# Indexer heads summed pair by pair as they are projected, and a query block's mask moved from a matrix product to GpSimd

## The chip, the cores and the metric

The kernel runs on one core of one Trainium2 chip. The metric is the device time of one execution in microseconds (us). Shorter is better. Engines are named as the profile names them: PE (matrix products), PEld (its weight loads), DVE (vector engine), ACT (scalar engine), POOL (GpSimd), SP (sync engine, which issues loads).

## What is computed

A trunk of two layers over 512 positions of width 1024: a gated linear recurrence, a feed-forward with a short convolution, a sparse attention, a second feed-forward, a final norm. The change lies in the sparse attention alone. Its reference, cut to what matters:

```
dots = jnp.einsum('bthd,bsd->bths', qib, k_idx)                       # 8 index heads of 64
scores = jnp.einsum('bths,bth->bts', jax.nn.relu(dots), wb)           # weighted sum over the heads
scores = jnp.where(admissible[None], scores, NEG_BIG)                 # causal
_, sel = lax.top_k(scores, top_k)                                     # top_k = 128 of up to 512 keys
logits = jnp.einsum('btkgd,btskd->btkgs', qb, k_sel) * (ATT_HEAD_DIM ** -0.5)
probs = softmax(where(valid, logits + bias, NEG_BIG))                 # 16 heads, relative-position bias
out = einsum('btkgs,btskd->btkgd', probs, v_sel)
```

The kernel gathers nothing. It computes all logits of a query block and adds a large number to the keys that were not selected.

## The kernel before

All work is in blocks of 128 queries (t = 0 to 3); block t sees (t + 1) * 128 keys. Every float32 product is made of three products of parts, so a projection of 128 columns (`proj_T`) is 8 steps of three matrix products, 24 in all. Weights pass through `wunit`: SP loads them, ACT writes the high part `whi` (L143 or L159) and ACT, DVE or POOL the low part `wlo`; in one form (L158 to L160) ACT writes a negated copy and POOL issues a load that adds to it. The buffers of `whi` and `wlo` are three deep.

The attention stage begins with the index key (KI, 72 columns: 64 of the key, 8 head weights), then four projections of the index queries (QI0 to QI3 here, two heads each; `head_in`), then K, V and eight pairs of query heads (q0 to q7; `rest_in`). `kw_evac` (L704 to L706) makes the two parts of the index key, and `kw_weights` transposes the head weights on PE (`pw`) and has DVE write `wN` (L715). After each QI projection `stack` splits its result into the two parts of both heads: ACT writes halves of `qh` and `ql` (L675, L676), DVE the other halves (L677, L678).

`dots` then runs for t = 1, 2, 3 and, inside that, for the four pairs of index heads: four matrix products into two banks `pi` (L749), a ReLU on ACT (L759) and a multiply-add on DVE into the score tile `sc[t]`, a part of `scs` (L755 and L760). POOL masks the diagonal block (L762). `top` finds the 128 largest by 16 rounds of MAX8 and MATCH_REPLACE8 on DVE (L774, L776), first for t = 1, then for t = 2 and 3, and writes the mask `sel[t]` (L779).

The attention itself goes in units (hf, b): head pair b and query blocks 0, 1 (hf = 0) or 2, 3 (hf = 1); six hf = 0 units come first, then both kinds mixed. `products` multiplies queries by keys into banks `pl` (L863). For t = 1 and t = 2 PE first adds the mask by a product of `sel[t]` with the identity (L860). For t = 3 POOL has added mask and bias beforehand (`mask3`, L833) into `scs`, which is free by then. `biased` (L870) is one DVE pass that adds the bias, or bias and mask, and takes the row minimum. ACT exponentiates (L889); `mixv` transposes the probabilities on PE (L912, L915), ACT copies them out (L916), and PE multiplies them by the values (L923, L926).

What sets the order: on PE the program's own order is kept. Pieces of work that run beside a projection are generators given to `add_side`; `weave` advances them by the PE time each step is reckoned at. The order on the other engines is made by the scheduler from when it reckons each operation ready, and each engine then works strictly through its own list.

Of the kernel before, what the change touches and what calls it, by code (L numbers as in the profile page):

```python
# [8 lines left out]
F32 = mybir.dt.float32  # L9
# [3 lines left out]
AF = mybir.ActivationFunctionType  # L13
ALU = mybir.AluOpType
# [3 lines left out]
P = 128  # L18
D = 1024
T = 512  # L20
# [3 lines left out]
NEG = -1e30  # L24
# [24 lines left out]
def trunk(ctx: ExitStack, tc: tile.TileContext, xT, vecs, convs, hgrn_w_in, hgrn_w_out, dsa_w_in, dsa_w_out,  # L49
# [11 lines left out]
    def bank(name):  # L61
        return ps.tile([P, 512], F32, name=name, tag="bank")
# [124 lines left out]
    def add_side(gen, rate=1.0):  # L187
        side.append([gen, rate, 0.0])
# [472 lines left out]
    with ExitStack() as sx:  # L661
# [9 lines left out]
        def stack(b, src, lo):  # L671

            a, c = qh[:, b, :], ql[:, b, :]
            top_, bot = rows2
            nc.scalar.activation(a[top_], src[top_], AF.Copy)  # L675
            nc.scalar.activation(c[bot], src[bot], AF.Copy)  # L676
            lo.tensor_tensor(a[bot], src[top_], a[top_].bitcast(F32), op=ALU.subtract)  # L677
            lo.tensor_tensor(c[top_], src[bot], c[bot].bitcast(F32), op=ALU.subtract)  # L678
# [9 lines left out]
        with ExitStack() as sy:  # L688
# [20 lines left out]
            def kw_weights():  # L709
                tmp = kw.pop()  # L710
                pw = bank("pw")
                for t in range(TT):
                    nc.tensor.transpose(pw[:, t * 72:(t + 1) * 72], tmp[:72, t * P:(t + 1) * P], ident[:72, :72])
                for t in range(TT):
                    nc.vector.tensor_scalar(wN[:, t, :], pw[:, t * 72 + 64:(t + 1) * 72], 8 ** -0.5 * 64 ** -0.5,  # L715
                                            rstd_c[:, t:t + 1], op0=ALU.mult, op1=ALU.mult)

            def setup():

# [13 lines left out]
            def head_in():  # L733
                pk = yield from proj_T(w_in, O_KI, 72)
                for b in range(4):
                    o = yield from proj_T(w_in, O_QI + b * P,
                                          hook=({7: lambda: kw_evac(pk)}, {2: kw_weights}, None, None)[b])
                    lo_engine[0] = nc.gpsimd
                    stack(4 + b, o, nc.vector)

            def dots():
                for t in range(1, TT):
                    w = (t + 1) * P
                    ts_ = slice(t * P, (t + 1) * P)
                    for b in range(4):
                        o = [bank("pi") for _ in range(2)]
                        for k_ in (ki_h, ki_l):
                            for e in range(2):
                                nc.tensor.matmul(o[e][:, :w], (qh, ql)[e][:, 4 + b, ts_], k_[:, :w],  # L749
                                                 start=k_ is ki_h, stop=k_ is ki_l)  # L750
                        yield 0.22 * (t + 1)
                        for e in range(2):
                            i = 2 * b + e
                            if i == 0:
                                nc.vector.tensor_scalar(sc[t], o[e][:, :w], 0.0, wN[:, t, 0:1],  # L755
                                                        op0=ALU.max, op1=ALU.mult)
                            else:
                                r_ = ix.tile([P, T], F32, name="relu", bufs=2)
                                nc.scalar.activation(r_[:, :w], o[e][:, :w], AF.Relu)  # L759
                                nc.vector.scalar_tensor_tensor(sc[t], r_[:, :w], wN[:, t, i:i + 1], sc[t],  # L760
                                                               op0=ALU.mult, op1=ALU.add)
                    nc.gpsimd.affine_select(sc[t][:, w - P:], sc[t][:, w - P:], pattern=[[-1, P]], base=0,  # L762
                                            channel_multiplier=1, compare_op=ALU.is_ge, fill=NEG)
                    done.add(f"sc{t}")
                    if t == 1:
                        add_side(top((1,)), 0.4)

            def top(ts):

                while any(f"sc{t}" not in done for t in ts):  # L770
                    yield 0.5
                for r in range(16):
                    for t in ts:
                        nc.vector.max(m8[:, t, :], sc[t])  # L774
                    for t in ts:
                        nc.vector.match_replace(sc[t], m8[:, t, :], sc[t], -3e38)  # L776
                    yield sum(2 * (0.065 + (t + 1) * P / 960) for t in ts)
                for t in ts:
                    nc.vector.tensor_scalar(sel[t], sc[t], -2e38, -NEG, op0=ALU.is_gt, op1=ALU.mult)  # L779
                    done.add(f"sel{t}")  # L780
                if 3 not in ts:
                    add_side(top((2, 3)), 0.55)
# [29 lines left out]
            add_side(norm_chain())  # L812
            add_side(setup())
            weave(head_in())
            add_side(dots(), 1.0)
            rest = rest_in()
            for c in rest:
                weave([c])
# [3 lines left out]
        at = sx.enter_context(tc.tile_pool(name="at", bufs=2))  # L822
        probs = {}

        def masked(b, e):
            return scs[:, e * T:e * T + T]

        def mask3(b):

            if b < KB and f"m{b}" not in done:  # L830
                done.add(f"m{b}")
                for e in range(2):
                    nc.gpsimd.tensor_tensor(masked(b, e), bias[:, 2 * b + e, :], sel[3], op=ALU.add)  # L833

        def scores(u):


            hf, b = u
            g = b // 4
            tiles = (2 * hf, 2 * hf + 1)  # L840
            if hf == 0:
                pb = [bank("pl") for _ in range(2)]
                ps_ = {(t, e): pb[e][:, t * 256:t * 256 + 256] for t in tiles for e in range(2)}
            else:
                ps_ = {}
            mn = [at.tile([P, 2], F32, name="mn", bufs=6) for e in range(2)]
            L = [[None, None], [None, None]]

            def products(t):
                w = (t + 1) * P  # L850
                wp = max(w, 256)
                ts_ = slice(t * P, t * P + P)
                if hf:
                    for e in range(2):
                        ps_[t, e] = bank("pl")
                if t == 3:
                    mask3(b)
                elif t:
                    for e in range(2):
                        nc.tensor.matmul(ps_[t, e][:, :w], identb, sel[t], start=True, stop=False)  # L860
                for k_ in (kh, kl):
                    for e in range(2):
                        nc.tensor.matmul(ps_[t, e][:, :wp], (qh, ql)[e][:, b, ts_], k_[g][:, :wp],  # L863
                                         start=t in (0, 3) and k_ is kh, stop=k_ is kl)

            def biased(j, t):
                w = (t + 1) * P
                for e in range(2):
                    L[e][j] = at.tile([P, 384 + j * P], F32, name=f"L{j}", bufs=4)
                    nc.vector.tensor_tensor_reduce(L[e][j][:, :w], ps_[t, e][:, :w],  # L870
                                                   masked(b, e) if t == 3 else bias[:, 2 * b + e, (3 - t) * P:],
                                                   scale=1.0,
                                                   scalar=3e38, op0=ALU.add, op1=ALU.min,
                                                   accum_out=mn[e][:, j:j + 1])

            for j, t in enumerate(tiles):
                products(t)
                if hf:
                    biased(j, t)
                yield (0.47, 0.66, 0.87, 0.92)[t]  # L880
            if hf == 0:
                for j, t in enumerate(tiles):
                    biased(j, t)
            sm = at.tile([P, 2, 2], F32, name="sm", bufs=4)
            rs = at.tile([P, 2, 2, 64], F32, name="rs", bufs=4)
            for e in range(2):
                for j, t in enumerate(tiles):
                    l = L[e][j][:, :(t + 1) * P]
                    nc.scalar.activation(l, l, AF.Exp, bias=mn[e][:, j:j + 1], scale=-1.0, accum_out=sm[:, j, e:e + 1])  # L889
            nc.vector.reciprocal(sm, sm)  # L890
            nc.vector.tensor_copy(rs, sm[:, :, :, None].to_broadcast([P, 2, 2, 64]))
            probs[u] = L, rs
            if {"sel3", "q8"} <= done:
                later = [c for f, c in units[units.index(u) + 1:] if f]
                mask3(later[0] if later else KB)
# [143 lines left out]
```

## Time and profile before

| | us |
|---|---|
| median of three runs | 1273.68 (1273.42 to 1275.24) |
| the profiled execution's own time | 1276.48 |
| its span, first to last instruction | 1274.7 |
| PE busy | 1251.4 (98%) |
| DVE busy | 803.0 (63%) |
| ACT busy | 599.6 (47%) |
| POOL busy | 138.8 (11%) |

The attention stage lies at 668 to 865 us of the span. Busy time is the union of an engine's instructions. A PE that is busy all the time in a stretch has no waits there; the time is then the sum of what it issues.

### The profile page before, as it was taken

Reading aid. Unit: us, or ns where it says so; the run is one execution under the profiler, and the core shown is the slowest. Engines: PE = TensorE matmul, PEld = TensorE weight load, DVE = VectorE, ACT = ScalarE, POOL = GpSimd, SP = SyncE. Lnnn points to the kernel's source line nnn. Section 1 sums busy time; section 2 is a strip of 40 time slices with the busy share of each in tenths; the row PEclk is TensorE's granted clock in tenths of the full one; section 3 lists DMA queues with packets and bytes.
Section 4 is the critical chain, followed back from the end, with each engine's and each line's share of the span. In section 5 each row is a group of like instructions: output and inputs, shape, how many; then the busy total and the mean of one; then the engine's idle time right before and its main releaser. Section 6 shows DMA issues by size and latency. Waiting matters only on the chain.

```text
span 1274.7 us, 15695 instructions
## 1 busy us (share of the span) xinstructions
PE 1251.4 (98%) x6054; PEld 1046.2 (82%) x6054; DVE 803.0 (63%) x1305; ACT 599.6 (47%) x989; POOL 138.8 (11%) x120
## 2 busy tenths in 40 slices
PE   8999999999999999999999998999999999999997
PEld 7788888887888888888887777988888888888887
DVE  7755777756777777742444999635677777762331
ACT  5546565444544444421337757853444444441430
POOL 3022223110000000000003453300000000000000
PEclk9999999999999999999999999999999999999999
DMA  6339777323333333322237850003233333333222
GB/s 199 117 73 158 133 129 126 76 66 99 91 93 98 99 99 99 98 91 93 87 103 173 134 109 25 27 1 99 83 100 99 99 99 94 92 95 99 91 75 66
DMA packets 199178, 124.05 MB, mean 97 GB/s; under 512 B 5264, under 2 KB 188480, under 8 KB 199104
## 3 DMA queue, kind: packets, MB, share of 16 engines
q1 hardware_dynamic: 170320, 108.31, 28.7%
q0 software_dynamic: 28080, 14.16, 9.3%
q8 instruction: 47, 0.77, 0.3%
q10 hardware_dynamic: 704, 0.58, 0.2%
q14 instruction: 27, 0.22, 0.1%
HBM read 120.92 MB, written 2.12 MB: 97 GB/s over the span
## 4 chain that ended last, share of the span: by engine, by line
PE 88%; DVE 7%; ACT 2%; issue 1%; DMA 0%; POOL 0%; DVEq 0%; SPq 0%; POOLq 0%; ACTq 0%
PE pj L169 17%; PE pj L171 17%; PE pj L170 17%; PE px L169 9%; PE px L171 9%; PE px L170 9%; PE pav L923 2%; DVE scs L776 2%; PE pl L556 1%; PE po L602 1%; DVE m L774 1%; DVE scs L760 1%; PE pl L863 1%; PE pt L912 1%; PE pn L170 1%
## 5 line engine op out<-in xcount | busy, mean ns | idle before, releaser
L169 PE MATMUL pj<-x,whi 128*128 128x512 f32 (+1 forms) x1016 | 403.0, 397 | 0.0
L171 PE MATMUL pj<-x,wlo 128*128 128x512 f32 (+1 forms) x1016 | 396.9, 391 | 1.1 <-DMA wlo<-in_dsa_w_in_dram 1.1
L170 PE MATMUL pj<-x,whi 128*128 128x512 f32 (+1 forms) x1016 | 396.3, 390 | 0.0
L144 DVE TENSOR_TENSOR wlo<-wr,whi 128x1024 fp32r<-128x1024 f32 (+2 forms) x165 | 202.0, 1224 | 155.1 <-ACT whi L143 153.1
L143 ACT ACTIVATE whi<-wr 128x1024 fp32r<-128x1024 f32 (+1 forms) x167 | 173.6, 1039 | 257.1 <-PE px L170 155.2
L171 PEld LDWEIGHTS pj<-x,wlo 128*128 128x128 f32 (+1 forms) x1016 | 190.6, 188 | 42.4 <-DMA wlo<-in_dsa_w_in_dram 1.5
L169 PEld LDWEIGHTS pj<-x,whi 128*128 128x128 f32 (+1 forms) x1016 | 191.0, 188 | 39.2 <-issue 1.6
L170 PEld LDWEIGHTS pj<-x,whi 128*128 128x128 f32 (+1 forms) x1016 | 191.1, 188 | 38.8 <-issue 1.0
L169 PE MATMUL px<-ah,whi 128*128 128x512 f32 (+1 forms) x332 | 128.5, 387 | 0.0
L171 PE MATMUL px<-ah,wlo 128*128 128x512 f32 (+1 forms) x332 | 127.5, 384 | 0.0
L170 PE MATMUL px<-al,whi 128*128 128x512 f32 (+1 forms) x332 | 126.2, 380 | 0.0
L348 DVE TENSOR_TENSOR ub<-pj,rstd_r 128x512 f32<-128x512 f32 x88 | 60.6, 688 | 82.3 <-PE pj L171 77.3
L143 ACT ACTIVATE ah<-c 128x512 fp32r<-128x512 f32 x44 | 27.8, 631 | 115.9 <-DVE c L360 115.9
L171 PEld LDWEIGHTS px<-ah,wlo 128*128 128x128 f32 x332 | 62.3, 188 | 13.5
L170 PEld LDWEIGHTS px<-al,whi 128*128 128x128 f32 x332 | 62.3, 188 | 12.8
L351 ACT ACTIVATE c<-ub,convc 128x512 f32<-128x512 f32 x88 | 71.2, 809 | 2.4 <-DVE ub L348 1.6
L169 PEld LDWEIGHTS px<-ah,whi 128*128 128x128 f32 x332 | 62.4, 188 | 11.4
L353 DVE SCALAR_TENSOR_TENSOR c<-ub,convc,c 128x512 f32<-128x512 f32 x88 | 66.2, 752 | 3.0
L358 ACT ACTIVATE c<-c 128x512 f32<-128x512 f32 x44 | 27.8, 632 | 80.8 <-DVE c L353 80.7
L352 DVE SCALAR_TENSOR_TENSOR c<-ub,convc,c 128x512 f32<-128x512 f32 x88 | 65.6, 746 | 0.0
L522 DVE TENSOR_TENSOR qk<-qk,ftree 128x512 f32<-128x512 f32 x56 | 39.6, 709 | 17.6 <-PE pl L560 7.1
L144 DVE TENSOR_TENSOR al<-c,ah 128x512 fp32r<-128x512 f32 x44 | 30.4, 692 | 29.3 <-ACT ah L143 29.3
(226 smaller groups left out, 1743.9 us busy)
## 6 DMA issues: line engine op xcount, KB each, us to landing
wr<-in_ffn_w_up_dram SPq DMA_DIRECT2D x88, 512.0 KB, 3.8
wr<-in_ffn_w_down_dram SPq DMA_DIRECT2D x41, 512.0 KB, 3.7
wr<-in_hgrn_w_in_dram SPq DMA_DIRECT2D x30, 512.0 KB, 4.1
wlo<-in_hgrn_w_in_dram POOLq DMA_DIRECT2D x19, 512.0 KB, 7.5
wr<-in_dsa_w_in_dram SPq DMA_DIRECT2D x14, 512.0 KB, 3.7
wr<-in_hgrn_w_out_dram SPq DMA_DIRECT2D x8, 512.0 KB, 3.6
wlo<-in_dsa_w_in_dram POOLq DMA_DIRECT2D x8, 512.0 KB, 7.8
wr<-in_dsa_w_out_dram SPq DMA_DIRECT2D x8, 512.0 KB, 3.8
```

Source lines behind the costliest of these rows:

```text
L143: nc.scalar.activation(dst_h, src, AF.Copy)
L144: lo.tensor_tensor(dst_l, src, dst_h.bitcast(F32), op=ALU.subtract)
L169: nc.tensor.matmul(o, ah, bh, start=start, stop=False)
L170: nc.tensor.matmul(o, ah, bl, start=False, stop=False)
L171: nc.tensor.matmul(o, al, bh, start=False, stop=stop)
L348: nc.vector.tensor_tensor(u[:, 2:], o, rows(), op=ALU.mult)
L351: nc.scalar.activation(c, u[:, 2:], AF.Identity, scale=cc[2], bias=cc[3])
L352: nc.vector.scalar_tensor_tensor(c, u[:, 1:T + 1], cc[1], c, op0=ALU.mult, op1=ALU.add)
L353: nc.vector.scalar_tensor_tensor(c, u[:, 0:T], cc[0], c, op0=ALU.mult, op1=ALU.add)
L358: nc.scalar.activation(g, g, AF.Silu)
L522: nc.vector.tensor_tensor(turned(m), turned(m), factors(ft, m), op=ALU.mult)
L776: nc.vector.match_replace(sc[t], m8[:, t, :], sc[t], -3e38)
```

## The change

Two edits. First, `dots` becomes `dots(b)`: one piece of side work for each pair of index heads, added as soon as the `stack` of that pair has been issued, with the loop over t inside. It starts once `wN` has been issued. The masking of the diagonal and `top((1,))` follow the last pair. Second, the mask of query block t = 2 is added to the bias by POOL, as that of t = 3 already was, into two new tiles `m20` and `m21`; the product with the identity stays for t = 1 alone.

```diff
+                done.add("wN")
...
                     stack(4 + b, o, nc.vector)
-
-            def dots():
+                    add_side(dots(b))
+
+            def dots(b):
+
+                while "wN" not in done:
+                    yield 0.3
                 for t in range(1, TT):
...
-                    for b in range(4):
...
+                    if b == 3:
+                        nc.gpsimd.affine_select(sc[t][:, w - P:], sc[t][:, w - P:], pattern=[[-1, P]], base=0,
...
-            add_side(dots(), 1.0)
...
-        def masked(b, e):
-            return scs[:, e * T:e * T + T]
+        masked2 = [at.tile([P, 3 * P], F32, name=f"m2{e}", bufs=1) for e in range(2)]
+
+        def masked(t, e):
+            return scs[:, e * T:e * T + T] if t == 3 else masked2[e]
...
-                for e in range(2):
-                    nc.gpsimd.tensor_tensor(masked(b, e), bias[:, 2 * b + e, :], sel[3], op=ALU.add)
+                for t in (2, 3):
+                    for e in range(2):
+                        nc.gpsimd.tensor_tensor(masked(t, e), bias[:, 2 * b + e, (3 - t) * P:], sel[t], op=ALU.add)
...
-                if t == 3:
+                if t >= 2:
                     mask3(b)
...
-                                                   masked(b, e) if t == 3 else bias[:, 2 * b + e, (3 - t) * P:],
+                                                   masked(t, e) if t >= 2 else bias[:, 2 * b + e, (3 - t) * P:],
```

Where the projections of the second and third pair of index queries meet, PE's list before is (`pj_5136` is QI1's result, `pj_5184` QI2's):

```order
L169 MATMUL pj_5136<-x_79,whi_5132 128x512
L170 MATMUL pj_5136<-x_81,whi_5132 128x512
L171 MATMUL pj_5136<-x_79,wlo_5133 128x512
L169 MATMUL pj_5184<-x_78,whi_5180 128x512
L170 MATMUL pj_5184<-x_80,whi_5180 128x512
L171 MATMUL pj_5184<-x_78,wlo_5181 128x512
L169 MATMUL pj_5184<-x_78,whi_5180 128x512
L170 MATMUL pj_5184<-x_80,whi_5180 128x512
```

In the changed kernel the same place on PE (`pj_5136` is again QI1, `pj_5214` is QI2; `qh` and `ql` are what `stack` writes) is:

```order
L169 MATMUL pj_5136<-x_79,whi_5132 128x512
L170 MATMUL pj_5136<-x_81,whi_5132 128x512
L171 MATMUL pj_5136<-x_79,wlo_5133 128x512
L169 MATMUL pj_5214<-x_78,whi_5210 128x512
L170 MATMUL pj_5214<-x_80,whi_5210 128x512
L171 MATMUL pj_5214<-x_78,wlo_5211 128x512
L753 MATMUL pi_5222<-ki_h_5032,qh_5012 128x256
L753 MATMUL pi_5223<-ki_h_5032,ql_5013 128x256
L753 MATMUL pi_5222<-ki_l_5033,qh_5012 128x256
L753 MATMUL pi_5223<-ki_l_5033,ql_5013 128x256
L753 MATMUL pi_5234<-ki_h_5032,qh_5012 128x384
L753 MATMUL pi_5235<-ki_h_5032,ql_5013 128x384
```

The first product of pair 1 has come to stand three matrix products behind the end of its own projection; it stands in the same place behind QI2 and QI3, and for pair 0 three products behind the transposes `pw`. Before, the products of all pairs stood behind QI3 and three products of K.

On ACT, around the splits of those projections, the list before reads (L159 and L158 are weight parts, L675 and L676 the halves of `stack`):

```order
L159 ACTIVATE whi<-wr 128x1024
L675 ACTIVATE qh<-pj 64x512
L676 ACTIVATE ql<-pj 64x512
L158 ACTIVATE wlo<-wr 128x1024
L159 ACTIVATE whi<-wr 128x1024
L675 ACTIVATE qh<-pj 64x512
L676 ACTIVATE ql<-pj 64x512
```

And in the changed kernel:

```order
L675 ACTIVATE qh<-pj 64x512
L676 ACTIVATE ql<-pj 64x512
L158 ACTIVATE wlo<-wr 128x1024
L763 ACTIVATE relu<-pi 128x256 x2
L763 ACTIVATE relu<-pi 128x384 x2
L763 ACTIVATE relu<-pi 128x512 x2
L159 ACTIVATE whi<-wr 128x1024
L675 ACTIVATE qh<-pj 64x512
L676 ACTIVATE ql<-pj 64x512
```

The six ReLUs of a pair now stand between two splits, and the weight part L159 still stands ahead of each split.

On POOL, in the hf = 1 units, the difference begins with these rows (`m_5598` and `m_5599` are the new tiles):

```order
-L833 TENSOR_TENSOR scs<-bias,sel_5021 128x512 x16
-L344 MEMSET ub_7187 128x2
-L344 MEMSET ub_7188 128x2
+L840 TENSOR_TENSOR m_5598<-bias,sel_5020 128x384
+L840 TENSOR_TENSOR m_5599<-bias,sel_5020 128x384
+L840 TENSOR_TENSOR scs<-bias,sel_5021 128x512 x2
+L840 TENSOR_TENSOR m_5598<-bias,sel_5020 128x384
+L840 TENSOR_TENSOR m_5599<-bias,sel_5020 128x384
+L840 TENSOR_TENSOR scs<-bias,sel_5021 128x512 x2
```

Two additions of 384 columns now stand ahead of the two of 512 columns, eight times over.

## Rows read from the trace of the kernel before

**Rows 1.** Stretches: length; busy of PE, PEld, DVE, ACT, POOL; clock; DMA.
```profile
684.00:699.00 15.00, 15.00 (x69) 12.42 (x68) 7.78 (x12) 8.78 (x12) 4.85 (x3) 1.00 0.65 127
716.00:740.00 24.00, 22.30 (x101) 17.89 (x100) 24.00 (x68) 15.58 (x21) 12.79 (x11) 1.00 0.96 153
785.00:790.00 5.00, 3.23 (x23) 2.81 (x23) 4.55 (x17) 3.09 (x11) 0.86 (x1) 1.00 0.00 0
800.00:840.00 40.00, 40.00 (x258) 36.67 (x257) 24.10 (x88) 34.51 (x94) 13.68 (x12) 1.00 0.04 13
```

**Rows 2.** PE's waits at 668 to 850: total us, times, longest.
```profile
PE pl L860 <- DVE sel L779: 3.9, 2, 2.1
...
PE pj L171 <- DMA wlo<-in_dsa_w_in_dram: 1.1, 1, 1.1
...
PE pt L796 <- DVE tmp L696: 0.6, 1, 0.6
```

**Rows 3.** Timeline of PE: start, us, engine, line, operation.
```profile
684.75 0.40 PE L169 MATMUL pj<-x,whi 128*128 128x512 f32 x1
...
699.06 0.28 PE L749 MATMUL pi<-ki_h,qh 128*128 128x256 f32 x1
...
701.89 0.28 PE L749 MATMUL pi<-ki_h,qh 128*128 128x256 f32 x1
702.26 0.36 PE L749 MATMUL pi<-ki_h,ql 128*128 128x256 f32 x1
```

**Rows 4.** Timeline of ACT behind the end of QI3, with idle time and releaser.
```profile
698.41 1.06 ACT L159 ACTIVATE whi<-wr 128x1024 fp32r<-128x1024 f32 x1 [2.08 <-issue]
699.48 0.59 ACT L675 ACTIVATE qh<-pj 64x512 fp32r<-64x512 f32 x1
700.08 0.59 ACT L676 ACTIVATE ql<-pj 64x512 fp32r<-64x512 f32 x1
```

**Rows 5.** Timeline of DVE: the index key's low part, then splits of the first and last pair.
```profile
683.77 2.47 DVE L705 TENSOR_TENSOR ki_l<-tmp,ki_h 64x512 fp32r<-64x512 f32 x1 [0.77 <-ACT ki_h L704]
...
687.34 0.68 DVE L677 TENSOR_TENSOR qh<-pj,qh 64x512 fp32r<-64x512 f32 x1
688.06 0.69 DVE L678 TENSOR_TENSOR ql<-pj,ql 64x512 fp32r<-64x512 f32 x1
...
700.71 0.69 DVE L677 TENSOR_TENSOR qh<-pj,qh 64x512 fp32r<-64x512 f32 x1 [0.60 <-ACT ql L676]
701.42 0.69 DVE L678 TENSOR_TENSOR ql<-pj,ql 64x512 fp32r<-64x512 f32 x1
```

**Rows 6.** The stretch behind PE's wait for the first mask; columns as in Rows 1.
```profile
743.60:747.20 3.60, 3.60 (x11) 2.82 (x10) 2.92 (x13) 1.97 (x8) 0.17 (x1) 0.53 0.91 113
```

**Rows 7.** Timeline of PE at the mask products of two hf = 1 units.
```profile
822.58 0.49 PE L860 MATMUL pl<-sel,identb 128*128 128x384 bf16 x2
...
829.31 0.49 PE L860 MATMUL pl<-sel,identb 128*128 128x384 bf16 x2
829.50 0.47 PE L863 MATMUL pl<-kh,qh 128*128 128x384 f32 x1
829.81 0.34 PE L863 MATMUL pl<-kh,ql 128*128 128x384 f32 x1
829.98 0.34 PE L863 MATMUL pl<-kl,qh 128*128 128x384 f32 x1
```

**Rows 8.** DVE's first MAX8 and the mask of block t = 1.
```profile
707.33 0.41 DVE L774 MAX8 m<-scs 128x8 f32<-128x256 f32 x1
...
741.83 0.73 DVE L779 TENSOR_SCALAR sel<-scs 128x256 bf16<-128x256 f32 x1
```

**Rows 9.** Timeline of POOL: a weight part, and additions of mask and bias.
```profile
683.29 2.39 POOL L144 TENSOR_TENSOR wlo<-wr,whi 128x1024 fp32r<-128x1024 f32 x1 [3.58 <-ACT whi L143]
...
793.35 2.14 POOL L833 TENSOR_TENSOR scs<-bias,sel 128x512 f32<-128x512 f32 x1
...
832.12 2.27 POOL L833 TENSOR_TENSOR scs<-bias,sel 128x512 f32<-128x512 f32 x2 [4.07 <-DVE mn L870]
```

More of the change, by code (lines that the diff above doesn't have):

```diff
@@ L744, in dots @@
                     ts_ = slice(t * P, (t + 1) * P)
-                    for b in range(4):
-                        o = [bank("pi") for _ in range(2)]
-                        for k_ in (ki_h, ki_l):
-                            for e in range(2):
-                                nc.tensor.matmul(o[e][:, :w], (qh, ql)[e][:, 4 + b, ts_], k_[:, :w],
-                                                 start=k_ is ki_h, stop=k_ is ki_l)
-                        yield 0.22 * (t + 1)
-                        for e in range(2):
[L753 to L766, printed above, removed]
+                    o = [bank("pi") for _ in range(2)]
+                    for k_ in (ki_h, ki_l):
+                        for e in range(2):
+                            nc.tensor.matmul(o[e][:, :w], (qh, ql)[e][:, 4 + b, ts_], k_[:, :w],
+                                             start=k_ is ki_h, stop=k_ is ki_l)
@@ new lines, in dots @@
+                    yield 0.22 * (t + 1)
+                    for e in range(2):
+                        i = 2 * b + e
+                        if i == 0:
+                            nc.vector.tensor_scalar(sc[t], o[e][:, :w], 0.0, wN[:, t, 0:1],
+                                                    op0=ALU.max, op1=ALU.mult)
+                        else:
+                            r_ = ix.tile([P, T], F32, name="relu", bufs=2)
+                            nc.scalar.activation(r_[:, :w], o[e][:, :w], AF.Relu)
+                            nc.vector.scalar_tensor_tensor(sc[t], r_[:, :w], wN[:, t, i:i + 1], sc[t],
+                                                           op0=ALU.mult, op1=ALU.add)
@@ L768, in top @@
+                    if b == 3:
+                        nc.gpsimd.affine_select(sc[t][:, w - P:], sc[t][:, w - P:], pattern=[[-1, P]], base=0,
+                                                channel_multiplier=1, compare_op=ALU.is_ge, fill=NEG)
+                        done.add(f"sc{t}")
+                        if t == 1:
+                            add_side(top((1,)), 0.4)
             def top(ts):
@@ L831, in mask3 @@
                 done.add(f"m{b}")
-                for e in range(2):
-                    nc.gpsimd.tensor_tensor(masked(b, e), bias[:, 2 * b + e, :], sel[3], op=ALU.add)
+                for t in (2, 3):
+                    for e in range(2):
+                        nc.gpsimd.tensor_tensor(masked(t, e), bias[:, 2 * b + e, (3 - t) * P:], sel[t], op=ALU.add)
         def scores(u):
@@ L863, in products @@
                         nc.tensor.matmul(ps_[t, e][:, :wp], (qh, ql)[e][:, b, ts_], k_[g][:, :wp],
-                                         start=t in (0, 3) and k_ is kh, stop=k_ is kl)
+                                         start=t != 1 and k_ is kh, stop=k_ is kl)
             def biased(j, t):
```

## Prediction

> **What bounds the kernel now.** I read the stretches first, then PE's waits, then the timelines of the engines around each wait. In the heart of the attention PE has no gap, 40.00 of 40 us, while DVE has 24.10 and POOL 13.68 [rows 1]: what PE no longer issues there is saved, and what PE waits anywhere is paid, unless a later wait shrinks by as much. Ahead of it the picture is another one. From 684 to 699, while the index queries are projected, DVE has 7.78 of 15 us; from 716 to 740 it is full, 24.00 of 24, and PE has gaps [rows 1]. PE's waits in the stage that this change can touch are two for masks, 3.9 us in all with 2.1 the longer and so 1.8 the other, 1.1 for a weight part that comes by a POOL load, and 0.6 for a scaled projection [rows 2]. Behind the 2.1 us wait the granted clock was 0.53 for 3.6 us, close to the lower level of 1.2 GHz [rows 6]: 3.6 x (1 - 0.53) = 1.7 us lost. Behind the 1.8 us wait the clock stayed at 1.00 in the stretch at 785 [rows 1].
>
> **The first edit, what it adds.** Nothing is removed: the same 48 index products, ReLUs and multiply-adds are issued. What moves is PE's place for them, and PE keeps its list. They need `qh` and `ql` of their pair, and those have a chain. Behind the end of QI3, ACT first runs the weight part L159 from 698.41, which takes 1.06, and only then the two halves of the split, from 699.48 and 700.08 [rows 4]; DVE adds the other halves at 700.71 and 701.42, and `ql` is complete at 701.42 + 0.69 = 702.11 [rows 5]. PE's product with it starts at 702.26 [rows 3], so the signal takes 0.15. L159 writes the weight buffer that the finished projection has just freed, so it cannot come sooner, and in the changed list it still stands ahead of the split.
>
> Before, this latency lay under the other pairs' products. In the changed list the first product of a pair stands three products behind its projection, the place that PE reached at 699.06 [rows 3] behind QI3. There it must wait for `qh`: 700.71 + 0.69 + 0.15 = 701.55, or 2.5 us [rows 5]. The second product waits for `ql` until 702.26, which is 3.2 behind 699.06; less the one product of 256 columns in between, 0.12 us (by columns from the 0.17 that separates two of 384 [rows 7]; 0.23 for 512), the pair waits 3.1 us. The same three ACT and two DVE operations follow QI1 and QI2, so pairs 1, 2 and 3 pay 3 x 3.1 = 9.3.
>
> Pair 0 has another chain. Its products stand three products behind the transposes `pw`, a place that PE reached at 684.75 [rows 3]. Its split waits on DVE behind the low part of the index key, which took 2.47 us at 683.77 where its like takes 0.7, in the same time as a weight part on POOL from 683.29 to 685.68 [rows 5, 9]. So `qh` is there at 687.34 + 0.68 + 0.15 = 688.17, a wait of 3.4, and `ql` at 688.06 + 0.69 + 0.15 = 688.90, 0.6 behind its product's turn at 688.29 [rows 5]. Pair 0 pays 4.0. The four come to 13.3; before, the last pair already lost 702.26 - 701.89 = 0.37 less 0.12, so 0.25, in this way [rows 3]. **Added: 13.0.** Nothing covers it: PE's next rows are products that stand behind the waiting one, and ACT, DVE and POOL have nothing that would need less time for it.
>
> The clock: four waits of 3.1 to 4.0 us are each longer than the one of 2.1 that cost 1.7. Two waits of about 2 us disagree [rows 1, 6], so the number of falls is open, from none to five (four pairs and the first mask) against one before. I take three: **2 x 1.7 = 3.4 more**, bounds -1.7 and +6.8. The Trainium skill, "TensorE: Matmul & The Clock Gate", section "HAM oscillation — how this bites in real kernels", says that a loop with repeated waits pays the return to half clock at each of them, not once. By that the sum would be higher by the two further falls, 3.4; the trace agrees for one wait of two.
>
> **The first edit, what it gives back.** DVE's sums begin some 15 us sooner, in time that it had free, so less stands between its first MAX8 and the mask, 707.33 to 742.56 before [rows 8]. But PE's list from the last pair to the mask product is full as well, 120 projection products of 0.23 us = 28 us, and the last pair's sums are themselves late by the waits above. In the changed list DVE has 6 multiply-adds there instead of 14, but three MAX8 and four MATCH_REPLACE8 of the later blocks more. So the 2.1 us wait may stay or go: I take **-1.0**, bounds 0 and -2.1. The wait of 1.8 for the masks of t = 2 and 3 goes: three hf = 0 units instead of six stand ahead of them on DVE, and PE no longer needs them for its products, only DVE does, later: **-1.8**. The weight part that came 1.1 late was queued on ACT behind ReLUs that are no longer there, and the 0.6 came from the full DVE: **-1.2** of 1.7, bounds 0 and -1.7.
>
> **The second edit.** Per hf = 1 unit it takes a pair of mask products off PE. They start at 829.31, the next product at 829.50, and that one is followed after 0.31 where the next spacing is 0.17 [rows 7]: 0.19 + 0.14 = 0.33 if the slower start goes too, 0.19 if it stays behind the transposes. Eight units: 1.5 to 2.6, **-2.2**. POOL gets two additions of 384 columns. Two of 512 take 2.27 [rows 9], so by columns 0.86 each, 1.7 a unit and 4.0 in all; a unit takes PE 829.31 - 822.58 = 6.7 us, now 0.3 less [rows 7], and the masks of the next unit are made while PE transposes. I cost it at nothing while that holds.
>
> **Sum.** 13.0 + 3.4 - 1.0 - 1.8 - 1.2 - 2.2 = +10.2. The profiled execution took 1276.48 us, so its like would take 1286.7; against the median of 1273.68 shown for before, which is 2.8 lower for the same work, the forecast is 1283.9.
>
> **Rivals.** *The earlier sums win.* If the splits came in time, all that is left of the sum is its gains: -2.2 for the mask products, -3.9 for both mask waits, -1.7 for the clock and -1.7 for the rest, -9.5, and the time is 1264.2. It decides at an average wait of 9.5 / 4 = 2.4 us per pair: below that the kernel is faster. For it speaks the half-empty DVE at 684 to 699; against it that the row at 702.26 shows PE waiting for just this split although two other pairs' products and six projection products had stood between. 0.08. *No measurable change:* the waits come to about 2.4 each, or no clock falls and all gains are full with a few waits shortened, 1271 to 1276.2. 0.06.
>
> *POOL's masks come too late.* `m20`, `m21` and `scs` exist once, so the masks of a unit start only when DVE has read those of the last, and where two hf = 1 units follow each other without an hf = 0 unit between, little time is left. One addition took 2.14 instead of 1.14 us [rows 9]. If all four did so, a unit's masks would take 4.0 x 2.14 / 1.14 = 7.5, 1.1 above PE's 6.4, and six units in a row would add 6: 1290. The Trainium skill, "SBUF — State Buffer", section "Who interferes with whom", gives the mechanism: POOL and a DVE operation with two SBUF inputs lock each other out for a whole instruction. The row at 793.35 bears that out, but DVE's pass over `pl` has one input in PSUM and is not of that kind. 0.08.
>
> **How the numbers follow.** The forecast, with waits of 3 to 4 us at each pair, has 0.78, and lies between 13.0 - 1.7 - 2.6 - 1.8 - 2.1 - 1.7 = +3.1 and 13.0 + 6.8 - 1.5 - 1.8 = +16.5: 1276.8 to 1290.2. With a little of the neighbouring cases the range is 1276.5 to 1291; it leaves out the faster case, the unchanged one and the ends. 0.2% is 2.5 us, about what a measurement of this kernel can tell from no change. Slower by more: the forecast and POOL's case, 0.86. Within it: 0.06. Faster: 0.08.
>
> **What would show it.** In the profile after, PE should wait in front of L753 four times, for DVE L678 or L677, about 13 us in all, with stretches of lower clock behind some; DVE should have its gaps there too. The wait for the masks of t = 2 and 3 should be gone, POOL should have 32 additions, and PE should stay without gaps in the hf = 1 units. The forecast is wrong if PE's waits at L753 come to under 9 us, or if PE waits for transposes' inputs behind late masks.

## The result: slower by 18.1 us, at the upper end of the range

| | before | after |
|---|---|---|
| median, us | 1273.68 (1273.42 to 1275.24) | 1291.82 (1287.59 to 1293.63, 4 runs) |
| the profiled execution's own time | 1276.48 | 1292.92 |
| its span | 1274.7 | 1291.1 |
| PE busy | 1251.4 | 1258.9 |
| DVE / ACT / POOL busy | 803.0 / 599.6 / 138.8 | 808.4 / 599.2 / 150.7 |

The ratio is 1.0135, with a 95% interval of 1.0108 to 1.0162. The forecast was 1283.9 with a range up to 1291.0. The median lies 0.8 us beyond that end; the ratio, which goes by the means, gives 1273.68 x 1.0135 = 1290.9, just inside. Four runs do not tell the two apart. The sign and the main mechanism were right; the size was 1.7 to 1.8 times the forecast. Between the two profiled executions the difference is 16.4 us, and that is what the terms below are added up against.

PE's waits in the attention stage, in the profile of after (engine, line, tile, what it waited for, us in total, times, longest), which answer [rows 2]:

```profile
PE pi L753 <- DVE qh L677: 9.1, 4, 2.8
PE pt L922 <- DVE rs L898: 2.4, 1, 2.4
PE pl L867 <- DVE sel L784: 2.1, 1, 2.1
PE pav L930 <- ACT px L923: 1.5, 3, 1.0
PE pi L753 <- DVE ql L678: 1.3, 4, 0.4
```

The four waits in front of the index products are there, as foreseen. They come to 9.1 + 1.3 = 10.4 us, above the 9 below which the prediction called itself wrong. The wait for the masks of t = 2 and 3 is gone, and so are the late weight part and the late `tmp`. The 2.1 us for the mask of t = 1 stayed. And there is a wait that the prediction did not have: 2.4 us for `rs`, the reciprocal rows that PE transposes.

PE's timeline at pairs 0 and 2 (start, duration, instruction, and in brackets the idle time before it), which answers [rows 3]:

```profile
684.37 0.40 PE L171 MATMUL pj<-x,wlo 128*128 128x512 f32 x1
687.54 0.58 PE L753 MATMUL pi<-ki_h,qh 128*128 128x256 f32 x1 [2.77 <-DVE qh L677]
688.36 0.55 PE L753 MATMUL pi<-ki_h,ql 128*128 128x256 f32 x1 [0.23 <-DVE ql L678]
...
692.13 0.63 PE L753 MATMUL pi<-ki_h,ql 128*128 128x512 f32 x1
692.55 0.63 PE L753 MATMUL pi<-ki_l,qh 128*128 128x512 f32 x1
...
708.12 0.39 PE L171 MATMUL pj<-x,wlo 128*128 128x512 f32 x1
710.60 0.58 PE L753 MATMUL pi<-ki_h,qh 128*128 128x256 f32 x1 [2.10 <-DVE qh L677]
711.42 0.55 PE L753 MATMUL pi<-ki_h,ql 128*128 128x256 f32 x1 [0.23 <-DVE ql L678]
```

The bracket counts from the modelled end of the product ahead. What PE really loses is counted by starts: the product ahead starts at 708.12 and takes 0.23 of PE's time, so the place is reached at 708.35 and left at 710.60, 2.25 us; the next product stands 0.82 behind where it should stand 0.12 behind, 0.70 more. That makes 2.95 us for pair 2, and pairs 1 and 3 have the same two waits. Pair 0 loses 687.54 - 684.60 = 2.94 and 0.70, together 3.64. The four come to 3.64 + 3 x 2.95 = 12.5. The two rows at 692 show the other part of the loss: these products start 0.42 apart where 0.23 is usual.

The chain behind a wait is the one that the prediction had read from [rows 4, 5]. ACT at pair 2, in after:

```profile
707.69 1.06 ACT L159 ACTIVATE whi<-wr 128x1024 fp32r<-128x1024 f32 x1 [3.36 <-issue]
708.65 0.57 ACT L675 ACTIVATE qh<-pj 64x512 fp32r<-64x512 f32 x1
709.24 0.59 ACT L676 ACTIVATE ql<-pj 64x512 fp32r<-64x512 f32 x1
```

and DVE behind it, idle for 4.38 us until ACT's second half was done:

```profile
709.86 0.68 DVE L677 TENSOR_TENSOR qh<-pj,qh 64x512 fp32r<-64x512 f32 x1 [4.38 <-ACT ql L676]
```

The granted clock in the stretches behind the waits (window, length, busy time and instructions of PE, PEld, DVE, ACT and POOL, granted clock, DMA share, GB/s), which answer [rows 6]: behind pairs 0, 1, 2 and 3, behind the mask of t = 1, behind the wait for `rs`.

```profile
688.00:693.00 5.00, 4.76 (x15) 4.09 (x15) 2.78 (x7) 0.88 (x2) 0.00 (x0) 0.50 0.03 10
699.00:703.50 4.50, 4.28 (x15) 3.66 (x16) 2.28 (x5) 1.90 (x5) 1.61 (x1) 0.64 0.81 150
711.00:716.00 5.00, 4.76 (x14) 4.07 (x14) 2.47 (x5) 1.56 (x4) 1.55 (x1) 0.50 0.87 157
724.00:727.00 3.00, 2.60 (x9) 2.40 (x10) 1.53 (x3) 1.18 (x4) 1.55 (x1) 0.52 0.55 153
759.00:763.00 4.00, 3.77 (x20) 3.21 (x20) 4.00 (x17) 3.94 (x10) 2.65 (x3) 1.00 1.09 201
799.00:802.00 3.00, 2.68 (x12) 2.13 (x11) 3.00 (x14) 2.90 (x12) 0.00 (x0) 0.54 0.03 4
```

0.50 is the lower level, 1.2 GHz. It fell behind all four pairs and behind `rs`, five times, but not behind the 2.13 us for the mask, where the profile of before shows its one fall behind a wait of 2.14. The five did not cost the same. Counted by starts (each distance between products less what the same product takes at clock 1.00) the four pairs lost 2.4, 1.6, 2.8 and 1.4 us, 8.1 together, and the fall behind `rs` 1.3: behind pairs 0 and 2 the clock stayed low about twice as long as behind 1 and 3.

Where `rs` was late, DVE and POOL were at work at the same time. DVE in after:

```profile
793.69 1.93 DVE L144 TENSOR_TENSOR wlo<-wr,whi 128x1024 fp32r<-128x1024 f32 x1
795.63 1.28 DVE L144 TENSOR_TENSOR ql<-on,qh 128x256 fp32r<-128x256 f32 x1
796.83 1.24 DVE L898 COPY rs<-sm 128x256 f32<-128x256 f32 x1
```

POOL beside it, the first four mask additions (two and two):

```profile
792.56 1.97 POOL L840 TENSOR_TENSOR m<-bias,sel 128x384 f32<-128x384 f32 x2 [0.35 <-POOL ql L678]
794.50 3.42 POOL L840 TENSOR_TENSOR scs<-bias,sel 128x512 f32<-128x512 f32 x2
```

and PE, which waits for it:

```profile
798.12 0.33 PE L922 MATMUL pt<-ident,rs 128*128 128x128 f32 x1 [2.41 <-DVE rs L898]
```

Three DVE operations took longer than their like does, 1.93, 1.28 and 1.24 us, until POOL was done at 797.92. That `rs` is late for this reason, and not because DVE is full of search rounds (it was busy for 10.00 of 10 us from 790 to 800), is only a reading here. An experiment below separates the two.

In the heart of the attention three hf = 1 units in a row begin in after at

```profile
839.26 0.42 PE L870 MATMUL pl<-kh,qh 128*128 128x384 f32 x1
...
845.88 0.42 PE L870 MATMUL pl<-kh,qh 128*128 128x384 f32 x1
...
852.30 0.42 PE L870 MATMUL pl<-kh,qh 128*128 128x384 f32 x1
```

so a unit takes (852.30 - 839.26) / 2 = 6.52 us, where it took 6.73 in [rows 7]: 0.21 less, 1.7 us for eight.

**The sum as it turned out.** Waits at the pairs 12.5, less the 0.25 of before: +12.2. Clock, five falls for one, by the starts 8.1 + 1.3 - 1.7: +7.7. Mask of t = 1: 0. Masks of t = 2 and 3: -1.8. Weight part and `tmp`: -1.7. Mask products: -1.7. The wait for `rs`: +2.4. The waits for `px`, 1.8 before and 1.5 after: -0.3. Together +16.8; the profiled executions differ by 16.4, so 0.4 us stay open. At the medians the difference is 18.1, since the profiled execution of before was 2.8 us above its median and that of after 1.1.

### The profile page after: what moved, and what is told of

It is laid out like the page before. It is cut to its first block, busy times and chain, and to the rows that moved or that the text cites. A ratio compares the mean times of both kernels' runs of the same rounds, so it can differ in the third digit from the quotient of the medians.

```text
span 1291.1 us, 15695 instructions
## 1 busy us (share of the span) xinstructions
PE 1258.9 (98%) x6038; PEld 1051.2 (81%) x6038; DVE 808.4 (63%) x1305; ACT 599.2 (46%) x989; POOL 150.7 (12%) x136
## 4 chain that ended last, share of the span: by engine, by line
PE 88%; DVE 6%; issue 2%; ACT 2%; POOL 0%; DMA 0%; DVEq 0%; SPq 0%; POOLq 0%; ACTq 0%
PE pj L170 16%; PE pj L169 16%; PE pj L171 16%; PE px L169 9%; PE px L171 9%; PE px L170 8%; PE pav L930 2%; PE pl L556 1%; DVE scs L781 1%; PE po L602 1%; PE pi L753 1%; PE pl L870 1%; DVE m L779 1%; PE pt L919 1%; DVE wlo L144 1%
```

## Experiments

In each, a line with + or - is against the changed kernel, if nothing else is said. The kernel before was timed again beside each group of runs, and had medians of 1274.68, 1274.42 and 1274.50 us.

### One edit at a time: the index products alone

```diff
-                for t in (2, 3):
-                    for e in range(2):
-                        nc.gpsimd.tensor_tensor(masked(t, e), bias[:, 2 * b + e, (3 - t) * P:], sel[t], op=ALU.add)
+                for e in range(2):
+                    nc.gpsimd.tensor_tensor(masked(b, e), bias[:, 2 * b + e, :], sel[3], op=ALU.add)
...
-                if t >= 2:
+                if t == 3:
                     mask3(b)
                 elif t:
```

> Only the first edit: index products pair by pair behind their projection; the masks of the third query block stay products on the tensor engine. Theory A (all of the loss is the first edit: PE waits in front of the index products, about 12.5 us, and the clock falls behind them, about 7.7 us): the four waits and their falls are there as in the changed kernel, 32 mask products come back (+2.2), POOL makes two additions per unit, not four, so the new wait of 2.4 us for the reciprocal rows (and its fall of about 1.3) goes: 1289 to 1293 us. Rival B (the second edit carries part of the loss beyond its new wait): below 1287 us.

Measured: 1290.42 us, ratio 1.0125 [1.0105, 1.0144]. PE waited 9.1 us for `qh` and 1.4 for `ql` in front of the index products, and 1.0 for `rs`. The time is theory A's: the first edit alone makes the loss, to within what these runs can tell. With two additions on POOL instead of four the wait for `rs` shrinks from 2.4 to 1.0 us. Theory A had it go; it does not, so this run leaves its cause open.

### One edit at a time: the masks alone

The index products as before, the masks of t = 2 on POOL as in the diff of the change.

> Only the second edit: the masks of the third query block are added to the bias on POOL; the index products stand where they stood before. Theory A: 16 pairs... of mask products go (-2.2 us), the 1.8 us wait for the masks of t=2 and 3 goes from PE, and the first four additions on POOL collide with DVE's weight part, split and reciprocal rows as in the changed kernel, which gives part back (+2.4 wait, +1.3 clock): 1270 to 1273.5 us, with DVE L144 and the copy of rs lengthened to above 1 us beside the POOL additions. Rival B (the wait for rs came from DVE being late after the first edit, not from the additions): no wait of PE for rs, 1269.7 us or a little less.

Measured: 1274.58 us, ratio 1.0004 [0.9995, 1.0014]: nothing, and 1 us above the upper end of theory A. There is no wait for `rs`; in its place PE waits 3.0 us for `px`. DVE's pass over the first masked unit shows why:

```profile
790.66 0.56 DVE L873 CUSTOM_DVE_ANT_0 L<-pl,m 128x384 f32<-128x384 f32 x1 [0.81 <-POOL m L836]
...
792.66 0.69 DVE L873 CUSTOM_DVE_ANT_0 L<-pl,scs 128x512 f32<-128x512 f32 x1 [0.56 <-POOL scs L836]
```

and PE's wait, with the stretch behind it:

```profile
796.22 0.70 PE L926 MATMUL pav<-px,vf 128*128 128x256 f32 x2 [2.95 <-ACT px L919]
```

```profile
796.00:800.00 4.00, 3.78 (x18) 3.73 (x19) 4.00 (x6) 2.91 (x12) 1.76 (x2) 0.61 0.00 0
```

DVE waits for each addition in turn; the exponentials on ACT wait for DVE; the copies `px` stand behind the exponentials on ACT; PE waits for `px` and then runs at a lower clock. So both theories missed the form. The first masks are needed as soon as `sel` is there, and four additions on POOL take some 5 us from that moment. What the later units save (1.7 us, and 1.8 for the wait on the masks) is spent on the first.

### The products 15 projection products later

```diff
                 while "wN" not in done:
                     yield 0.3
+                yield 3.6
```

> Both edits, but each pair's index products are recorded 15 projection products (3.4 us) later, 18 behind the projection instead of 3. Theory A (the waits are the latency of the split and nothing else): the waits of PE for qh and ql fall from 10.4 to under 1.5 us, no clock fall stands behind them, and the time falls by 18 to 22 us from the changed kernel's 1291.8, to 1270 to 1274 us, about the kernel before or a little below it. Rival B (what PE waits for is DVE, ACT and POOL throughput, so that the wait moves with the place or turns up at the masks): above 1280 us, with the same sum of waits at L753 or a longer one for sel1.

Measured: 1272.79 us, ratio 0.9983 [0.9975, 0.9992]: 19.0 us below the changed kernel. No wait for `qh` or `ql` is left, and the clock is 1.00 from 680 to 740; its one fall in the stage stands behind the mask of t = 1. The longest waits in the stage:

```profile
PE pl L868 <- DVE sel L785: 2.6, 1, 2.6
PE pav L931 <- ACT px L924: 2.4, 3, 1.2
```

Theory A holds. The loss at the pairs was the latency of the split, and moving PE's place by 3.4 us removes it. Not all of the 19.0 us is theirs: the wait for `rs` fell to 0.3 as well, while the one for `px` grew from 1.5 to 2.4 and that for the mask from 2.1 to 2.6. The same kernel is 0.17% faster than before.

### PE kept busy through the wait

```diff
                     o = [bank("pi") for _ in range(2)]
+                    if t == 1:
+                        for _ in range(13 if b else 16):
+                            nc.tensor.matmul(o[0], ki_h[:, :P], ki_h, start=True, stop=True)
```

> Both edits, and in front of each pair's first index product PE runs products that nobody reads, 16 for pair 0 and 13 for pairs 1 to 3, of 0.227 us each (3.6 and 2.95 us), about as long as the wait. The waiting is thus as long as in the changed kernel, but PE runs through it. Theory A (about 7.7 us of the loss is the clock that falls in the four waits): granted clock 1.00 from 684 to 745, and 1291.8 - 7.7 = 1284 us, 1282.5 to 1286. Rival B (the clock falls for another reason, or what the falls cost is small): 1289 us or more.

Measured: 1285.12 us, ratio 1.0085 [1.0072, 1.0098], 6.7 us below the changed kernel. These 55 products take 55 x 0.227 = 12.5 us, as long as the waits that they cover, and the clock stays up:

```profile
684.00:690.00 6.00, 6.00 (x33) 4.99 (x32) 5.57 (x9) 2.03 (x5) 1.97 (x1) 1.00 0.32 87
690.00:700.00 10.00, 10.00 (x48) 8.41 (x47) 5.78 (x11) 5.78 (x11) 1.61 (x1) 1.00 0.16 39
...
720.00:745.00 25.00, 25.00 (x114) 20.66 (x113) 24.83 (x73) 15.80 (x22) 11.43 (x11) 1.00 0.94 160
```

Theory A holds. This is the most direct measure of the clock's part, as the waits for the mask and for `rs` and the fall behind `rs` are there as in after: 6.7 us for four falls, 6.9 between the two profiled executions, 1.7 each on average. It is not a sharp one. By the two ratios it is 6.4, give or take 3.8 (both intervals taken together), which holds the 8.1 us by the starts as well.

### The products 6 projection products later

```diff
+                yield 1.8
```

> Both edits, with each pair's index products 6 projection products (1.36 us) later than in the changed kernel, where the run before this one had 15. If the waits are pure latency, each shrinks by 1.36 us: PE loses 2.3 us at pair 0 and 1.6 us at each other pair, 7.1 instead of 12.5. Theory A (each wait brings the clock down, short or long): four falls stay, 1291.8 - 5.4 = 1286.4 us, 1285 to 1288. Rival B (waits under 2 us do not bring it down): one fall or none of the four stays, 1279 to 1282 us.

Measured: 1277.63 us, ratio 1.0028 [1.0019, 1.0037], 14.2 us below the changed kernel. In front of pairs 0, 2 and 3 the waits shrank by 1.3 to 1.4 us, as expected. Pair 1 has none for `qh` left, since four index products of pair 0 now stand ahead of it too:

```profile
PE pi L754 <- DVE qh L677: 3.0, 3, 1.5
...
PE pi L754 <- DVE ql L678: 1.3, 3, 0.4
```

and the clock stayed at 1.00 from 680 to 780, also behind the 1.5 us. None of the four falls stayed, which is rival B's case. By starts the four pairs lose 2.35, 0.63, 1.59 and 1.60, 6.2 instead of 12.5. So of the 14.2 us, 6.3 are the shorter waits and 6.7 (8.1 by the starts) the falls that did not come. The time is below both theories' numbers, because pair 1 gained more than was reckoned and the wait for the mask of t = 1 shrank too, from 2.1 to 1.5; the one for `rs` went, but 2.3 for `px` stood in its place, with a fall behind it.

### The split without the weight part ahead of it

```diff
-            nc.scalar.activation(a[top_], src[top_], AF.Copy)
-            nc.scalar.activation(c[bot], src[bot], AF.Copy)
+            if dve:
+                nc.vector.tensor_copy(a[top_], src[top_])
+                nc.vector.tensor_copy(c[bot], src[bot])
+            else:
+                nc.scalar.activation(a[top_], src[top_], AF.Copy)
+                nc.scalar.activation(c[bot], src[bot], AF.Copy)
...
-                    stack(4 + b, o, nc.vector)
+                    stack(4 + b, o, nc.vector, True)
```

> Both edits, products three behind the projection as in the changed kernel, but the two halves of the split that ACT writes behind its weight part (1.06 us) are written by DVE, which is free then. If the wait is the chain ACT L159 1.06, L675 0.57, L676 0.57, DVE 0.68, then three DVE operations of about 0.68 take its place: qh 0.85 us sooner at each pair, PE's waits for qh 9.1 - 3.4 = 5.7 us. Theory A (and with waits that short the clock stays up, as it did with the products 6 later): 1291.8 - 3.4 - 6.7 = 1281.7 us, 1280 to 1283.5. Rival B (the weight part on ACT is not what the split waits for, or the DVE copies from PSUM take as long): 1287 us or more.

Measured: 1284.41 us, ratio 1.0084 [1.0070, 1.0097], 7.4 us below the changed kernel, between the theories. DVE at pair 2:

```profile
702.64 0.68 DVE L676 CAST qh<-pj 64x512 fp32r<-64x512 f32 x1 [2.12 <-PE pj L171]
703.36 0.69 DVE L677 CAST ql<-pj 64x512 fp32r<-64x512 f32 x1
704.08 0.68 DVE L681 TENSOR_TENSOR qh<-pj,qh 64x512 fp32r<-64x512 f32 x1
```

The operations stand 0.72 apart where ACT's stood 0.59 apart, so the idle time at pairs 1 to 3 went from 2.10 to 1.63 us, half of what was expected. Counted by starts the waits at the pairs are 2.1 us shorter. The larger part of the gain is the clock again, though not where the length of the wait would put it. Behind the 1.63 us of pair 1, and behind the same 1.63 us of pair 2:

```profile
694.00:698.00 4.00, 4.00 (x13) 3.53 (x14) 2.20 (x4) 1.61 (x4) 1.13 (x1) 0.57 1.07 194
705.00:709.00 4.00, 3.63 (x18) 3.07 (x19) 2.69 (x5) 2.25 (x5) 1.55 (x1) 1.00 0.86 166
```

One of the four falls was left, behind 1.63 us; behind the 2.62 us of pair 0 there was none. On the other side, here the clock fell behind the 2.14 us for the mask of t = 1, where in after it had not.

### The first masks on DVE

```diff
-                        nc.gpsimd.tensor_tensor(masked(t, e), bias[:, 2 * b + e, (3 - t) * P:], sel[t], op=ALU.add)
+                        (nc.gpsimd if b else nc.vector).tensor_tensor(masked(t, e), bias[:, 2 * b + e, (3 - t) * P:], sel[t], op=ALU.add)
```

This was made in three kernels. In the one with the masks alone:

> Only the second edit, as in the run that gave 1274.58 us, but the four mask additions of the first unit with query blocks 2 and 3 are done by DVE, not POOL; the other seven units stay on POOL. Theory A (the second edit's gain was eaten by those first four additions, which PE reaches within 2 us of the mask and which POOL makes at 1 to 1.5 us each): the wait of 3.0 us for the transposed probabilities and the clock fall behind it go or fall below 1 us, 1270 to 1272.5 us. Rival B (POOL is too slow or in DVE's way in the later units as well): 1274 us or more, with waits of PE behind 800 us.

Measured: 1272.00 us, ratio 0.9985 [0.9976, 0.9994], where POOL's additions gave 1.0004. The 3.0 us for `px` are gone (1.3 in two waits are left, and 1.7 for `rs`), and the clock is 1.00 from 680 on. Theory A holds. With the masks in time for the first unit, the second edit is worth 2.4 us by the medians and 1.9 by the ratio (0.8 to 3.1).

In the kernel with the late products:

> Both edits with the index products 15 projection products later (1272.79 us), and the first unit's four mask additions on DVE instead of POOL. In the run without this the PE waits behind the masks were small (0.3 us for rs, 0.4 for mn, and 2.4 for px, part of which is in the kernel before too). Theory A (POOL's first additions lock DVE): rs, ql and wlo on DVE at their usual 0.28, 0.42 and 1.2 us, 1271 to 1272.5 us. Rival B (DVE is full there, and four more additions of 2.5 us in all on it cost as much as the lock): 1273 to 1275 us.

Measured: 1270.53 us, ratio 0.9973 [0.9964, 0.9982]. This is the fastest of all, 3.9 us below the kernel before and 2.3 below the same kernel with the additions on POOL; by the ratios the last is 1.3, with intervals that overlap. Theory A's time is met and passed, its picture only in part: `rs` took 0.28 us, but `wlo` took 2.19 and `ql` 1.28 us, now beside POOL's additions for the second unit (785.22 to 790.24). PE did not wait for them.

In the changed kernel itself, to settle the wait for `rs`:

> The changed kernel with only the first unit's four mask additions on DVE instead of POOL. Theory A (the wait of 2.4 us for rs comes from POOL's additions, beside which DVE's wlo, ql and rs took 1.93, 1.28 and 1.24 us): these are back at 1.2, 0.42 and 0.28, the wait is under 0.5 us, and the time 1285 to 1290 us. Rival B (DVE is full there with the rounds of the search, and rs is late for that): the wait stays at 2 us or more, 1290 to 1293 us.

Measured: 1287.64 us, ratio 1.0101 [1.0082, 1.0120]. PE has no wait for `rs`. DVE's list is no emptier there, it has the four additions as well; but with no POOL addition beside them its operations are short:

```profile
791.69 0.28 DVE L898 COPY rs<-sm 128x256 f32<-128x256 f32 x1
791.89 0.41 DVE L144 TENSOR_TENSOR ql<-on,qh 128x256 fp32r<-128x256 f32 x1
...
797.27 1.22 DVE L144 TENSOR_TENSOR wlo<-wr,whi 128x1024 fp32r<-128x1024 f32 x1
```

0.28, 0.41 and 1.22 us against 1.24, 1.28 and 1.93: together 2.5 us shorter, as much as the wait of 2.4. The wait came with POOL's additions, not with the search rounds, as theory A had it. The scheduler also puts `wlo` behind `rs` here, and no run separates that order from the durations; but by the sum the durations alone are enough.

### The first unit of the attention later

What the late products leave is 2.6 us for the mask of t = 1. With `yield 6.0` ahead of the first unit's scores PE comes to it 18 projection products later:

> Both edits with the index products 15 projection products later, and PE's first unit of the attention, the one that waits 2.6 us for the mask of t=1, 18 projection products (4.1 us) later, between other projections. Theory A: the wait and the clock fall behind it go: 1272.8 - 2.6 - 1.7 = 1268.5 us, 1267.5 to 1269.5. Rival B (the units that follow now come too close upon each other, and DVE and ACT fall behind): the wait turns up at px, rs or mn near 770 us, 1271 us or more.

Measured: 1272.82 us, ratio 0.9987 [0.9978, 0.9996], as without it. The wait for the mask is gone, and this has come for it:

```profile
PE pav L931 <- ACT px L924: 5.2, 2, 2.9
```

Half the way (`yield 3.0`, with the first masks on DVE):

> Both edits with the index products 15 projection products later and the first unit's four mask additions on DVE (1270.53 us), and PE's first unit of the attention 9 projection products (2.0 us) later. With 18 products and the additions on POOL this brought nothing, since PE then waited 5.2 us for px in place of 2.6 for the mask. Theory A (half the way the mask of t=1 is nearly in time and the later units are not yet pushed together): the mask wait falls from 2.7 to about 0.7 and its clock fall goes, 1267 to 1269 us. Rival B (DVE is full from 720 to 790 us, so that any wait taken from the mask comes back at px or rs): 1270 us or more.

Measured: 1271.60 us, ratio 0.9978 [0.9968, 0.9987], no better than the 1270.53 without it: 0.6 us for the mask, 4.6 for `px`. Rival B holds in both. DVE has no gap from 730 to 770 in either, and PE's waits there are moved about, not removed.

## Why the prediction came out as it did

**The waits at the four pairs** were forecast at 13.3 us and measured at 12.5. The chain was read rightly, the weight part on ACT, two halves, two subtractions, each with its duration. (In the kernel before, three other pairs' products and nine projection products stood ahead of the row at 702.26, not two and six as the prediction says of it; the argument gains by that.) Pair 0 was taken 0.4 too long, the others 0.15. The kernels with later products confirm that it is latency: 15 products later no wait is left, 6 products later those of pairs 0, 2 and 3 are shorter by about the 1.36 us that these take, and that of pair 1 by more.

**The clock** was the step that failed in size. Three falls were assumed for four waits and the mask, +3.4 us; there were five, and by the starts they cost 7.7 more than the one of before, beyond the bound of 6.8. The price of one, 1.7 us by [rows 6], was about right on average (6.7 / 4 = 1.7 by the filled waits, 2.0 by the starts), but it came from a single fall, and single ones cost from 1.3 to 2.8. The number of falls was the guess, and it was taken from the middle of its bounds although each wait, as forecast, was longer than the one that had cost a fall. The Trainium skill, "TensorE: Matmul & The Clock Gate", section "HAM oscillation — how this bites in real kernels", says of a kernel whose clock falls in each of its repeated waits that the return is paid every time, not once. By that the term would have been 3.4 higher, +6.8; the count of five came out in this execution, though with a fall behind `rs` in place of the one behind the mask. That it is not so in every execution is what the four runs of after suggest: 1293.63 and 1292.92 us at mean clocks of 0.988 and 0.987, 1290.72 at 0.989, 1287.59 at 0.992. Only the run of 1292.92 has a trace, so that the number of falls makes this spread is not shown.

**The wait for `rs`**, 2.4 us, was not in the sum. The prediction named the mechanism, POOL's additions beside DVE, as the rival "POOL's masks come too late", but looked for it in the wrong place. It weighed the units in the heart of the attention, where PE stays without gaps and that rival did not come. It passed over the first unit, where `sel` is ready only just before its use and where DVE's operations (`wlo`, `ql`, `rs`) are not the pass over `pl` that it had checked. "I cost it at nothing while that holds" should have had the first unit as its exception. This wait and its fall, 2.4 + 1.3 = 3.7 us, are more than half of the 6.2 us by which +10.2 fell short of the 16.4 between the profiled executions. The second of the prediction's signs of being wrong, a wait for what PE transposes, thus came in part: PE waited for `rs`, not behind late masks but behind DVE operations that the making of the masks had drawn out.

**The mask of t = 1** was to shrink by 1.0 and did not. The search did become shorter, 31.4 us from the first MAX8 to the mask (727.76 to 759.18) against 35.2 in [rows 8], but PE's list moved as well: from `pw` to that unit PE had 195 projection products before, 189 after, 207 with the late products, since by the program the unit starts once the search has been issued. Read so, a wait whose place is tied to its cause need not shrink when the cause comes sooner; no run separates this.

**The rest** came out: the masks of t = 2 and 3 -1.8 as forecast, the weight part and `tmp` -1.7 (forecast -1.2, bound -1.7), the mask products -1.7 (forecast -2.2, bounds -1.5 to -2.6).

**The rivals.** "The earlier sums win" was refused by the place of the products alone: with the wait under the decision point of 2.4 us per pair (6.2 / 4 = 1.5 with 6 products) the kernel is still slower, 1277.63. That point was reckoned with all gains full, and the `rs` or `px` wait and the mask of t = 1 held some of them back. With no wait at the pairs it is faster, by 0.17 and 0.27%.

## What to carry to other kernels

Work that depends on the result of the step just ahead belongs as many instructions behind it as the chain to its operands lasts: 3 products behind cost 18 us here, 18 products behind gained 2, and doing without the wait was worth more than covering it with products that nobody reads (1272.79 against 1285.12). A move that lets one engine begin earlier is paid by the engine that keeps strict order, and each such wait of PE can be paid a second time at the lower clock, 1.3 to 2.8 us here where it fell. When work is handed to POOL, look at the first item apart from the steady run: it is the one with no lead.

## What the runs showed of the hardware

The length of a wait alone did not tell whether the clock fell. It fell behind waits of 2.1 to 2.8 us at all four pairs of after, behind one of three waits of 1.63 in the kernel with the split on DVE, and not behind its 2.62. In the changed kernel with the first masks on DVE it fell behind pairs 1 and 3 and not behind pair 2, with 2.10 us at each. Behind 1.49 us, with the products 6 later, it did not fall. The plainest case is the wait for the mask of t = 1, which is 2.13 or 2.14 us long in eight of the profiles: the clock fell behind it in five (before, the products alone, the masks alone, the split on DVE, the changed kernel with the first masks on DVE) and not in three (after, the filled waits, the masks alone with the first on DVE).

A POOL addition lengthened DVE operations with a single input as well: the copy `rs` took 1.24 us instead of 0.28, and the mask `sel` of t = 3, written at 792.69 beside POOL's first additions, 1.08 instead of the 0.41 that it took with no addition on POOL. The Trainium skill, "SBUF — State Buffer", section "Who interferes with whom", counts copies, if their operands meet certain conditions, among the operations that can take the ports shared with GpSimd, besides those with two SBUF inputs; the 1.24, 1.28 and 1.93 us beside POOL and the 0.28, 0.41 and 1.22 without it agree with both.
